# Norm writes ordered behind the next tile's residual sums, and k-interleaving kept only for the last tile of a stage head, in an eight-core encoder kernel

## The chip, the cores and the metric

The kernel runs on all 8 cores of one Trainium2 chip. Each core computes one element of the batch, and the cores exchange nothing. The metric is device time in microseconds (us) of the slowest core.

Runs come in two states. In the fast state the executions of one kernel agree within about 0.3%. In the slow state one die (four cores) or both show a lower granted TensorE clock and the time is some per cent longer; this comes and goes with any kernel. A ratio is the mean time of one kernel's fast runs over that of the other kernel's fast runs of the same rounds on the same chip, so it is not quite the ratio of the medians that are quoted. "Same" means within 2%.

Engines: PE is TensorE's matmul part, PEld its weight load, DVE is VectorE, ACT is ScalarE, POOL is GpSimd. PSUM has eight banks here, each holding one 128 x 512 fp32 block, the output of one block of matmuls.

## The reference, cut to what matters

```python
def rms_norm(x, g):
    y = x * lax.rsqrt(jnp.mean(x * x, axis=-1, keepdims=True) + EPS)
    return y * g

def sq_relu_mlp(h, w_up, w_down):               # 1024 -> 4096 -> 1024
    a = jax.nn.relu(h @ w_up)
    return (a * a) @ w_down

def short_conv_mixer(h, w_in, conv_w, w_out):   # 1024 -> 3 x 1024 -> 1024
    b, c, u = jnp.split(h @ w_in, 3, axis=-1)
    u = c * u
    # ... y = width-3 convolution of u along the sequence ...
    return (b * y) @ w_out

for i in range(2):                              # x is (8, 2048, 1024)
    h = rms_norm(x, norm_mix[i])
    x = x + (dilated_attention_mixer(h, ...) if i == 0 else short_conv_mixer(h, ...))
    x = x + sq_relu_mlp(rms_norm(x, norm_mlp[i]), *mlp_params[i])
return rms_norm(x, final_norm)
```

Every norm sits between two big matrix products: nothing of the next product can start on a token before that token's norm is done, and the norm can't start before the last residual sum of that token.

## The kernel before

Each core holds its 2048 tokens in four tiles of 512 tokens, with features on the partitions: a tile of x is eight blocks of 128 x 512 fp32 in SBUF. One output block of a 1024-wide product is eight matmuls of 128 x 512, which take about 1.73 us (8 x 216 ns) at full clock.

The kernel issues through its own list scheduler. It collects operations with their reads and writes, and places them engine by engine: of the operations that its cost model holds ready, the one with the lowest priority number, then with the lowest index. Each engine then executes in exactly that order, and waits where something isn't ready. The cost model knows durations.

```python
# in the scheduler: of the operations ready at time t on engine e
if o.ready <= t and (pick is None or (o.pri, o.idx) < (pick.pri, pick.idx)):
    pick = o
```

A norm of a tile is eight squares (on ACT, some on DVE), seven additions on GpSimd, one "ones-matmul" on PE that sums over the partitions and spreads the sum to all of them (bank 7), two activations that make the factor `rsqrt(mean + eps)`, and eight scalar_tensor_tensor instructions on DVE, `x * gain * factor`, that write the normalized tile `hT` in bf16. I call these eight "norm writes".

```python
def square_sum(gidx, src, c0, n, bank):
    for c in range(8):
        ...                                     # square of block c, on ACT or DVE
        if c:
            TT("pool", d, acc.ap[:, 0:n], o, ALU.add, ...)      # 7 adds on GpSimd, SBUF + SBUF
    MMS([(PS(bank, 0, n), onesN, h_ap(0, c0, n), True, True)], ...)   # the ones-matmul

def norm_tile(gidx, src, c0, n, bank, out_fn, pool=False, on_pe=True):
    ...
    nb_ = nrs[ni[0] % 2]
    rs = nb_.ap[:, 0:n]
    ACT(rs, PS(bank, 0, n), AF.Ln, ..., bias=eps_ap)
    ACT(rs, rs, AF.Exp, ..., scale=-0.5)        # the factor, in SBUF
    for c in range(8):
        out_fn(gidx, c, c0, n, src(c), nb_)     # norm_to_hT below, the final norm differs

def norm_to_hT(gidx, c, c0, n, src, nb_):
    STT(h_ap(c, c0, n), src[0], gain, nb_.ap[:, 0:n], ALU.mult, ALU.mult, ...)   # DVE

def add_x(tt, c, lo, n, b):                     # residual sum
    TT("dve", xa, xa, PS(b, 0, n), ALU.add, ...)    # DVE, SBUF + PSUM
```

In a stage head (the first products after a norm) each tile runs "k-interleaved": all four output blocks of the tile advance together, one 128-deep slice of `hT` after the other, so the tile can start when the first norm write is there. The price is that four of the seven banks fill at the same time and are finished at the same time.

```python
main = _Ring(range(7))                          # PSUM banks 0-6 in turn, 7 is the norm's

for tt in range(4):                             # head of the MLP
    bks = [main.next() for _ in range(4)]
    if pr == 0 and i == 0:
        for kc in range(8):
            MMS([(PS(bks[fc]), W[:, kc, ...], h_ap(kc, tt * 512, 512), kc == 0, kc == 7)
                 for fc in range(4)], ...)      # k-interleaved
    for fc in range(4):
        if pr or i:
            MMS([... for kc in range(8)], ...)  # bank by bank
        ACT(r.ap, PS(b), AF.Relu, ...)
        TT("pool", aT..., r.ap, r.ap, ALU.mult, ...)
```

Of the kernel before, what the change touches and what calls it, by code (L numbers as in the profile page):

```python
# [258 lines left out]
def build_nc():  # L259
# [22 lines left out]
    with ExitStack() as st:  # L282
# [12 lines left out]
        p = Prog()  # L295
# [26 lines left out]
        def ACT(out, in_, func, R, W, n, scale=None, bias=None, ps=True):  # L322
            kw = {}
            if scale is not None:
                kw["scale"] = scale
            if bias is not None:
                kw["bias"] = bias
            return p.op("act", lambda e: e.activation(out=out, in_=in_, func=func, **kw), R, W,  # L328
                        c_act(n, ps) + (0.09 if scale is not None and not isinstance(scale, float) else 0))
# [108 lines left out]
                    TT("pool", d, acc.ap[:, 0:n], o, ALU.add, [acc.r(0, n), r_], [dr], n)  # L438
            MMS([(PS(bank, 0, n), onesN, h_ap(0, c0, n), True, True)], [CR1, h_r(0, c0, n)], [PR(bank)])

        def norm_tile(gidx, src, c0, n, bank, out_fn, pool=False, on_pe=True):

            if not on_pe:
                square_sum(gidx, src, c0, n, bank)
            for c in range(8 if on_pe else 0):
                xa, xr = src(c)
                o, r_ = h_ap(c, c0, n), h_r(c, c0, n)
                alts = [("act", lambda e, o=o, i=xa: e.activation(out=o, in_=i, func=AF.Square), c_act(n, False)),  # L448
                        ("dve", lambda e, o=o, i=xa: e.tensor_tensor(out=o, in0=i, in1=i, op=ALU.mult),  # L449
                         c_dve(n, False))]  # L450
                if pool:
                    alts.append(("pool", alts[1][1], 0.2 + 0.0019 * n))
                p.op(alts, None, [xr], [r_], None)
                MMS([(PS(bank, 0, n), onesN, o, c == 0, c == 7)], [CR1, r_], [PR(bank)])
            nb_ = nrs[ni[0] % 2]
            ni[0] += 1
            rs = nb_.ap[:, 0:n]
            ACT(rs, PS(bank, 0, n), AF.Ln, [PR(bank), sm.r()], [nb_.r(0, n)], n, bias=eps_ap)
            ACT(rs, rs, AF.Exp, [nb_.r(0, n)], [nb_.r(0, n)], n, scale=-0.5, ps=False)
            for c in range(8):  # L460
                out_fn(gidx, c, c0, n, src(c), nb_)

        def norm_to_hT(gidx, c, c0, n, src, nb_):
            STT(h_ap(c, c0, n), src[0], sm.ap[:, S_GN + gidx * 8 + c:S_GN + gidx * 8 + c + 1],
# [416 lines left out]

        main = _Ring(range(7))

        def norm_x(gidx, tt, lo, n, fn):
            norm_tile(gidx, lambda c: xs(tt, c, lo, n), tt * 512 + lo, n, 7, fn, on_pe=n < 512)

        for tt in range(4):
            p.pri = 8000 + 10 * tt
# [22 lines left out]
        def mlp(l, base, tiles, tail):  # L911
            for pr in range(4):
                p.pri = base + 100 * pr
                fgs = (2 * pr, 2 * pr + 1)
                WU = [next_slot(wup_d[l][:, f * 512:(f + 1) * 512], 8, 512) for f in fgs]
                WD = [next_slot(wdn_d[l][f * 512:(f + 1) * 512, :], 4, 1024) for f in fgs]
                for i in range(2):
                    W, wb = WU[i]
                    for tt in range(4):
                        bks = [main.next() for _ in range(4)]  # L920
                        if pr == 0 and i == 0:
                            for kc in range(8):
                                MMS([(PS(bks[fc]), W[:, kc, fc * 128:(fc + 1) * 128], h_ap(kc, tt * 512, 512),
                                      kc == 0, kc == 7) for fc in range(4)],
                                    [wb.r(), h_r(kc, tt * 512, 512)], [PR(b) for b in bks])
                        for fc in range(4):
                            b = bks[fc]
                            if pr or i:
                                MMS([(PS(b), W[:, kc, fc * 128:(fc + 1) * 128], h_ap(kc, tt * 512, 512),
                                      kc == 0, kc == 7) for kc in range(8)],  # L930
                                    [wb.r()] + h_all(tt * 512, 512), [PR(b)])
                            r = rb_[ri[0] % 3]
                            ri[0] += 1
                            ACT(r.ap, PS(b), AF.Relu, [PR(b)], [r.r()], 512)
                            lo = fc * 2048 + tt * 512
                            TT("pool", aT[i].ap[:, lo:lo + 512], r.ap, r.ap, ALU.mult, [r.r()],
                               [aT[i].r(lo, lo + 512)], 512)
                p.pri = base + 100 * pr + 50
                for (tt, lo, n) in (tiles if pr == 3 else [(t_, 0, 512) for t_ in range(4)]):
                    c0 = tt * 512 + lo  # L940
                    for oc in range(8):
                        b = main.next()
                        MMS([(PS(b, 0, n), WD[i][0][:, fc, oc * 128:(oc + 1) * 128],
                              aT[i].ap[:, fc * 2048 + c0:fc * 2048 + c0 + n], i == 0 and fc == 0, i == 1 and fc == 3)
                             for i in range(2) for fc in range(4)],
                            [WD[0][1].r(), WD[1][1].r()] +
                            [aT[i].r(fc * 2048 + c0, fc * 2048 + c0 + n) for i in range(2) for fc in range(4)],
                            [PR(b)])
                        add_x(tt, oc, lo, n, b)
                    if pr == 3:  # L950
                        tail(tt, lo, n)

        mlp(0, 10000, [(t_, 0, 512) for t_ in range(4)], lambda tt, lo, n: norm_x(2, tt, lo, n, norm_to_hT))
# [13 lines left out]
        for i in range(8):  # L967
            p.pri = 20000 + 100 * i
            W, wb = next_slot(win_d[i], 8, 384)
            v, bs_ = vb[i % 2], bsb[i % 2]  # L970
            for tt in range(4):
                banks = [main.next() for _ in range(3)]
                parts = list(zip(banks, (128, 256, 0)))
                for ks, ps_ in ([((kc,), parts) for kc in range(8)] if i == 0 else
                                [(range(8), [q]) for q in parts]):
                    MMS([(PS(b), W[:, kc, coff:coff + 128], h_ap(kc, tt * 512, 512), kc == 0, kc == 7)
                         for (b, coff) in ps_ for kc in ks],
                        [wb.r()] + [h_r(kc, tt * 512, 512) for kc in ks], [PR(b) for (b, _) in ps_])
                cs = csb[ci % 2]
                ci += 1  # L980
                CP(cs.ap, PS(banks[0]), [PR(banks[0])], [cs.r()], 512, ("act",))
                lo = 1 + tt * 512
                TT("dve", v.ap[:, lo:lo + 512], cs.ap, PS(banks[1]), ALU.mult,
                   [cs.r(), PR(banks[1])], [v.r(lo, lo + 512)], 512)
                CP(bs_.ap[:, tt * 512:(tt + 1) * 512], PS(banks[2]), [PR(banks[2])],
                   [bs_.r(tt * 512, (tt + 1) * 512)], 512, ("act",))
            cw = [sm.ap[:, S_CW + k * 8 + i:S_CW + k * 8 + i + 1] for k in range(3)]
            for tt in range(4):
                y = yb[tt]
                o = tt * 512  # L990
                ACT(y.ap, v.ap[:, o:o + 512], AF.Copy, [v.r(o, o + 512), sm.r()], [y.r()], 512, scale=cw[0], ps=False)
                for k in (1, 2):
                    STT(y.ap, v.ap[:, o + k:o + k + 512], cw[k], y.ap, ALU.mult, ALU.add,
                        [v.r(o + k, o + k + 512), sm.r(), y.r()], [y.r()], 512)
                TT("pool", zT.ap[:, i * 2048 + o:i * 2048 + o + 512], bs_.ap[:, o:o + 512], y.ap, ALU.mult,
                   [bs_.r(o, o + 512), y.r()], [zT.r(i * 2048 + o, i * 2048 + o + 512)], 512)
        WO = [next_slot(wout_d[k * 512:(k + 1) * 512, :], 4, 1024) for k in range(2)]
        for tt in range(4):
            p.pri = 21000 + 10 * tt
            for oc in range(8):  # L1000
                b = main.next()

                def mm(kc):
                    return (PS(b), WO[kc // 4][0][:, kc % 4, oc * 128:(oc + 1) * 128],
                            zT.ap[:, kc * 2048 + tt * 512:kc * 2048 + tt * 512 + 512], kc == 0, kc == 7)

                def zr(kc):
                    return zT.r(kc * 2048 + tt * 512, kc * 2048 + tt * 512 + 512)

                MMS([mm(kc) for kc in range(7)], [WO[0][1].r(), WO[1][1].r()] + [zr(kc) for kc in range(7)], [PR(b)])  # L1010
                MMS([mm(7)], [WO[1][1].r(), zr(7)], [PR(b)])
                add_x(tt, oc, 0, 512, b)
            norm_x(3, tt, 0, 512, norm_to_hT)


# [108 lines left out]
```

## Time and profile before

| | value |
|---|---|
| time | 1524.02 us median of 3 runs (1523.65 to 1526.97) |
| span of the slowest core in the profile | 1523.8 us (core 7) |
| PE busy | 1454.9 us, 95% |
| DVE / POOL / ACT busy | 602.4 / 520.4 / 490.8 us |
| PE's share of the chain that ended last | 89% |

These are the lines of the profile's page for the kernel before: the span, the busy times, the shares of the chain that ended last, then two of the costliest groups. A group's line gives engine, operation, output<-input, shapes and count, then busy time and mean ns of one instruction, then the engine's idle time just before and its main releaser.

```profile
span 1523.8 us, 20000 instructions; the slowest of 8 cores (1516.7 to 1523.8 us)
...
PE 1454.9 (95%) x7207; PEld 674.7 (44%) x7207; DVE 602.4 (40%) x819; ACT 490.8 (32%) x778; POOL 520.4 (34%) x492
...
PE 89%; DVE 3%; DMA 3%; issue 2%; ACT 1%; POOL 1%; SPq 0%; DVEq 0%; ACTq 0%; POOLq 0%
...
L317 PE MATMUL psum<-arena 128*128 128x512 bf16 (+6 forms) x7207 | 1454.9, 366 | 61.1 <-ACT arena L448 18.3
...
L336 DVE SCALAR_TENSOR_TENSOR arena<-arena 128x512 bf16<-128x512 f32 (+2 forms) x232 | 181.6, 840 | 29.7 <-ACT arena L328 24.9
...
```

PE is the bottleneck, and it is idle for 61 us in all. L336 is 232 scalar_tensor_tensor instructions, 840 ns on average: the 136 norm writes that the change moves, 32 of the first norm and 64 of the convolution's taps. Where PE waits, once the start and the attention are over, is told by its waits between 310 and 1492 us (engine and line, what it waited for: us in total, times, longest):

```profile
...
engine line waited for: us in total, times, longest us
PE psum L317 <- ACT arena L328: 9.8, 6, 3.7
PE psum L317 <- DVE arena L333: 1.2, 1, 1.2
PE psum L317 <- POOL arena L333: 0.5, 1, 0.5
PE psum L317 <- POOL arena L965: 0.3, 1, 0.3
```

The 9.8 us behind L328 (the Relu; it frees PSUM banks) lie in the heads of the two MLPs. The timeline of the first one's head shows how they arise. A line gives start, duration, engine, line, operation and count, and in brackets the idle time before it and its releaser:

```profile
...
379.55 8.02 DVE L336 SCALAR_TENSOR_TENSOR arena<-arena 128x512 bf16<-128x512 f32 x8
...
387.49 1.27 DVE L333 TENSOR_TENSOR arena<-arena,psum 128x512 f32<-128x512 f32 x2
388.31 1.23 ACT L433 ACTIVATE arena<-arena 128x512 f32<-128x512 f32 x2 [10.09 <-DVE arena L333]
...
390.17 8.97 PE L317 MATMUL psum<-arena 128*128 128x512 bf16 x33 [2.23 <-ACT arena L328]
...
400.03 7.07 PE L317 MATMUL psum<-arena 128*128 128x512 bf16 x32 [0.90 <-ACT arena L328]
...
408.11 4.26 PE L317 MATMUL psum<-arena 128*128 128x512 bf16 x19 [1.00 <-ACT arena L328]
...
```

Read it from the top. DVE runs the eight norm writes of one tile in one block of 8.0 us (379.55). Only then come the last two residual sums of the next tile (387.49, x2). Read matmul by matmul, the products of these two sums had ended at 379.0 and 380.9 us. The squares of that tile start late accordingly (388.31, after ACT had been idle for 10.09 us). The Relus that give PE its banks back stand behind these squares in ACT's order, so PE stands for 2.23 us. The 33 matmuls after it take 8.97 us, where the 32 matmuls of the next line take 7.07: part of them ran at half clock. The waits of 0.90 and 1.00 us have another cause: the k-interleaved tile before gave back all its banks at once.

### The profile page before, as it was taken

How to read it: one execution, taken by the hardware profiler on the slowest of the kernel's cores; microseconds unless marked ns; L12 is line 12 of the kernel's file. 1: busy time of each engine (PE TensorE's matmuls, PEld its weight loads, DVE VectorE, ACT ScalarE, POOL GpSimd, SP SyncE). 2: the span in 40 equal slices, each digit the busy share in tenths (PEclk: the TensorE clock that was granted, in tenths of full speed). 3: DMA queues.
4: the chain of work that ended last, by engine and by line, in shares of the span. 5: the costliest groups of instructions: out<-in, count | busy, mean ns of one | idle time of the engine just before them, and what ended most of it. 6: DMA issues, size and time to landing. Idle time of an engine off the chain costs nothing.

```text
span 1523.8 us, 20000 instructions; the slowest of 8 cores (1516.7 to 1523.8 us)
## 1 busy us (share of the span) xinstructions
PE 1454.9 (95%) x7207; PEld 674.7 (44%) x7207; DVE 602.4 (40%) x819; ACT 490.8 (32%) x778; POOL 520.4 (34%) x492
## 2 busy tenths in 40 slices
PE   5999997699899999999999999999999999999996
PEld 2656443233344444444444444443444444444444
DVE  3646677557314013023038534457123023032057
ACT  3566686343220310310333433333310310301333
POOL 5100000135550530630665322246621621612552
PEclk8999999589999999999999999999999999999998
DMA  9944445630330420510410333311310411313014
GB/s 249 188 91 97 95 106 113 183 79 1 56 55 1 72 40 1 83 29 5 72 22 7 56 42 49 56 28 26 58 28 14 71 28 29 55 28 52 5 55 166
DMA packets 60911, 95.00 MB, mean 62 GB/s; under 512 B 3792, under 2 KB 40912, under 8 KB 58768
## 3 DMA queue, kind: packets, MB, share of 16 engines
q0 software_dynamic: 52016, 69.18, 26.6%
q1 hardware_dynamic: 8800, 24.55, 5.5%
q8 instruction: 60, 0.98, 0.3%
q14 instruction: 35, 0.29, 0.1%
HBM read 127.37 MB, written 8.52 MB: 89 GB/s over the span
## 4 chain that ended last, share of the span: by engine, by line
PE 89%; DVE 3%; DMA 3%; issue 2%; ACT 1%; POOL 1%; SPq 0%; DVEq 0%; ACTq 0%; POOLq 0%
PE psum L317 89%; DVE arena L336 3%; DMA arena<-scr 2%; DMA arena<-xT 2%; ACT arena L328 1%; DVE arena L333 1%; POOL arena L333 0%; POOL arena L349 0%; ACT arena L343 0%; ACT arena L433 0%; SPq L349 0%; DMA scr<-arena 0%; POOL arena L449 0%; DVE arena L345 0%; DVEq L216 0%
## 5 line engine op out<-in xcount | busy, mean ns | idle before, releaser
L317 PE MATMUL psum<-arena 128*128 128x512 bf16 (+6 forms) x7207 | 1454.9, 366 | 61.1 <-ACT arena L448 18.3
L317 PEld LDWEIGHTS psum<-arena 128*128 128x128 bf16 (+2 forms) x7207 | 674.7, 101 | 841.0 <-issue 155.5
L333 DVE TENSOR_TENSOR arena<-arena,psum 128x512 f32<-128x512 f32 (+1 forms) x384 | 258.2, 684 | 782.6 <-PE psum L317 776.1
L333 POOL TENSOR_TENSOR arena<-arena 128x512 bf16<-128x512 bf16 (+2 forms) x393 | 443.0, 1133 | 340.0 <-ACT arena L328 151.7
L328 ACT ACTIVATE arena<-psum 128x512 bf16<-128x512 f32 (+1 forms) x306 | 201.4, 669 | 639.0 <-PE psum L317 618.6
L336 DVE SCALAR_TENSOR_TENSOR arena<-arena 128x512 bf16<-128x512 f32 (+2 forms) x232 | 181.6, 840 | 29.7 <-ACT arena L328 24.9
L333 DVE TENSOR_TENSOR arena<-arena 128x2048 bf16<-128x2048 bf16 (+4 forms) x146 | 127.9, 921 | 35.3 <-ACT arena L328 25.7
L349 POOL DMA_DIRECT2D arena<-wdn x16 | 12.5, 784 | 318.9 <-PE psum L317 318.9
L433 ACT ACTIVATE arena<-arena 128x512 f32<-128x512 f32 x114 | 70.6, 631 | 153.4 <-DVE arena L333 136.2
L343 ACT CAST arena<-psum 128x512 bf16<-128x512 f32 (+2 forms) x149 | 87.2, 592 | 92.4 <-PE psum L317 87.7
L328 ACT ACTIVATE arena<-arena 128x512 f32<-128x512 f32 (+2 forms) x85 | 54.5, 659 | 65.3 <-DVE arena L333 51.0
L349 POOL DMA_DIRECT2D arena<-xT x18 | 13.4, 770 | 90.8 <-DVE arena L333 71.5
L349 POOL DMA_DIRECT2D arena<-wqk x8 | 7.4, 930 | 86.0 <-PE psum L317 86.0
L343 ACT COPY arena<-psum 128x512 f32<-128x512 f32 x38 | 22.9, 602 | 39.3 <-PE psum L317 39.2
L345 DVE CAST arena<-psum 128x512 bf16<-128x512 f32 (+2 forms) x27 | 18.4, 683 | 40.9 <-PE psum L317 40.7
L349 POOL DMA_DIRECT2D arena<-wup x16 | 15.0, 937 | 44.5 <-PE psum L317 39.7
L536 ACT ACTIVATE arena<-arena 128x1024 bf16<-128x1024 bf16 x23 | 24.1, 1059 | 1.9 <-DVE arena L345 0.7
L328 ACT ACTIVATE arena<-psum,arena 128x512 f32<-128x512 f32 (+1 forms) x29 | 19.5, 672 | 15.2 <-PE psum L317 14.9
L349 POOL DMA_DIRECT2D arena<-wo x8 | 4.3, 549 | 52.1 <-PE psum L317 52.1
L449 POOL TENSOR_TENSOR arena<-arena 128x512 bf16<-128x512 f32 x8 | 10.8, 1362 | 20.0 <-DMA arena<-xT 20.0
L448 ACT ACTIVATE arena<-arena 128x512 bf16<-128x512 f32 (+1 forms) x30 | 14.1, 523 | 9.2 <-DVE arena L333 7.0
L349 POOL DMA_DIRECT2D arena<-win x8 | 7.5, 932 | 14.8 <-PE psum L317 10.4
(16 smaller groups left out, 38.5 us busy)
## 6 DMA issues: line engine op xcount, KB each, us to landing
arena<-wup POOLq DMA_DIRECT2D x16, 1024.0 KB, 9.9
arena<-wdn POOLq DMA_DIRECT2D x16, 1024.0 KB, 12.8
arena<-xT POOLq DMA_DIRECT2D x14, 1024.0 KB, 9.8
arena<-arena SPq DMA_DIRECT2D x14, 512.0 KB, 4.6
arena<-scr SPq DMA_DIRECT2D x14, 512.0 KB, 6.4
arena<-win POOLq DMA_DIRECT2D x8, 768.0 KB, 7.5
outT<-arena SPq DMA_DIRECT2D x24, 256.0 KB, 2.5
arena<-wqk POOLq DMA_DIRECT2D x7, 512.0 KB, 10.0
```

What stands on the lines that cost most here:

```text
L317: i = e.matmul(o, lhsT=l, rhs=r, start=s0, stop=s1, skip_group_check=True)
L328: return p.op("act", lambda e: e.activation(out=out, in_=in_, func=func, **kw), R, W, c_act(n, ps) + (0.09 if scale is not None and not is ...
L333: return p.op(eng, lambda e: e.tensor_tensor(out=out, in0=in0, in1=in1, op=op), R, W, cost)
L336: return p.op("dve", lambda e: e.scalar_tensor_tensor(out=out, in0=in0, scalar=scalar, in1=in1, op0=op0, op1=op1), R, W, c_dve(n, False) + ...
L343: alts.append(("act", lambda e: e.copy(out=out, in_=in_), c_act(n) + more))
L345: alts.append((e_, lambda e: e.tensor_copy(out=out, in_=in_), c_dve(n, False) + more))
L349: return p.op(eng, lambda e: e.dma_start(out=out, in_=in_), R, W, 1.3 if eng == "sp" else 1.0, chan=chan, fill=fill, nbytes=nbytes)
L433: p.op([("act", lambda e, o=o, i=xa: e.activation(out=o, in_=i, func=AF.Square), c_act(n, False)), ("dve", lambda e, o=o, i=xa: e.tensor_t ...
L448: alts = [("act", lambda e, o=o, i=xa: e.activation(out=o, in_=i, func=AF.Square), c_act(n, False)), ("dve", lambda e, o=o, i=xa: e.tensor ...
L449: ("dve", lambda e, o=o, i=xa: e.tensor_tensor(out=o, in0=i, in1=i, op=ALU.mult), c_dve(n, False))]
L536: ("act", lambda e, o=sq.ap[:, sl], i_=rw.ap[:, sl]: e.activation(out=o, in_=i_, func=AF.Square), c_act(1024, False))], None, [rw.r(*rr)], ...
```

## The change

Intent: (A) the norm writes get a priority number 11 higher, so the scheduler orders them behind the next tile's residual sums; (B) only the last tile of a stage head stays k-interleaved, the other three run bank by bank, so that banks come free one at a time; (C) each tile of a down or output product gets its own priority step, which makes (A) work there too. No operation is added or removed.

```diff
-        def norm_tile(gidx, src, c0, n, bank, out_fn, pool=False, on_pe=True):
+        def norm_tile(gidx, src, c0, n, bank, out_fn, pool=False, on_pe=True, after=0):
 ...
+            p.pri += after
             for c in range(8):
                 out_fn(gidx, c, c0, n, src(c), nb_)
+            p.pri -= after
 ...
-            norm_tile(gidx, lambda c: xs(tt, c, lo, n), tt * 512 + lo, n, 7, fn, on_pe=n < 512)
+            norm_tile(gidx, lambda c: xs(tt, c, lo, n), tt * 512 + lo, n, 7, fn, on_pe=n < 512, after=11)
 ...
-                        if pr == 0 and i == 0:
+                        inter = pr == 0 and i == 0 and tt == 3
+                        if inter:
 ...
-                            if pr or i:
+                            if not inter:
 ...
-                p.pri = base + 100 * pr + 50
-                for (tt, lo, n) in (tiles if pr == 3 else [(t_, 0, 512) for t_ in range(4)]):
+                for k, (tt, lo, n) in enumerate(tiles if pr == 3 else [(t_, 0, 512) for t_ in range(4)]):
+                    p.pri = base + 100 * pr + 50 + 10 * k
 ...
                     if pr == 3:
+                        p.pri += 5
                         tail(tt, lo, n)
 ...
-                for ks, ps_ in ([((kc,), parts) for kc in range(8)] if i == 0 else
+                for ks, ps_ in ([((kc,), parts) for kc in range(8)] if i == 0 and tt == 3 else
 ...
                 add_x(tt, oc, 0, 512, b)
+            p.pri += 5
             norm_x(3, tt, 0, 512, norm_to_hT)
```

## The prediction

> **What bounds it now.** TensorE. The page shows it busy 1454.9 of 1523.8 us (95%), and 89% of the chain of waits. The change can only remove TensorE's idle time after 308 us and what follows from it. The timeline of the slowest core, read matmul by matmul, shows where that idle time is:
> - head of the first MLP (380-411 us): 2.2 + 0.9 + 1.0 = 4.1 us;
> - head of the convolution (825-842): 0.5 + 1.25 + 0.3 = 2.1 us;
> - head of the second MLP (1054-1085): 3.7 + 0.9 + 1.0 = 5.6 us;
> - the last stage: 1.1 us before the last tile's matmuls, then 14.8 us from the last down matmul (1509.1) to the end.
>
> **Why.** In each stage head VectorE runs eight scalar_tensor_tensor (0.66 us each alone, 1.7 us while a GpSimd add runs; block 379.6-387.5 us) in one block, and only then the last two residual sums of the next tile (387.5, 388.1), though their matmuls ended at 379.0 and 380.9. That tile's squares, GpSimd adds, norm and the PSUM banks wait for it. The 0.9-1.0 us gaps have another cause: a k-interleaved tile claims four of seven banks at once and finishes all four together, so the next one waits for a Relu (0.6 us). The second MLP's head also runs at half clock after its 3.7 us gap (33 matmuls take 9.8 us instead of 7.1); on five of eight cores the first MLP's does too (9.0). The Trainium skill ("TensorE: Matmul & The Clock Gate", What's actually happening) says an idle window of about 3.4 us halves the clock; this trace agrees for 3.7 us and shows it on some cores even after 2.2 us.
>
> **What the change does.** No operation is added or removed. The order of instructions shows residual sums and norm writes alternating on VectorE, the last tile's sum of squares some 6 us earlier, and tiles 0-2 of each head bank by bank. Both kinds of gap should go; the last tile still needs its norm, but 21 us of matmuls (3 x 6.9) stand before it.
>
> **Costs.** The norm writes now run among GpSimd's adds. The skill ("SBUF — State Buffer", Who interferes with whom) says a VectorE instruction with two SBUF inputs and a GpSimd one that reads SBUF exclude each other; the 0.66 against 1.7 us agrees. A pair (sum 0.6, write 0.66, wait about 0.4) comes to 1.7 us, just TensorE's 1.73 us per output block, so I expect a lag of 1-2 us, not a growing one. The small ones-matmul of the last norm is placed 5.2 us (convolution, second MLP) or 6.9 us (first MLP) into the head; my count from the trace's durations has it ready after about 4.5-5.5 us. I allow 2 us of new waits in all, at these ones-matmuls.
>
> **Sum.** Heads: 11.8 idle + about 3.5 clock. End: 1.1 (bank wait) + about 4 (the last half tile's eight sums now precede the other writes; before, VectorE reached them 4.5 us late; after, the output issues at about 0.45 us each limit). Minus 2 us. Net about 17-18 us, nearly all on the critical path, since TensorE is that path: **1506.5 us**, 8 in 10 within 1500 to 1515. Chances: faster by over 2% 0.02, within 2% 0.97, slower 0.01.
>
> **What would show it.** Right: gaps over 0.3 us at the heads nearly gone; no half clock near 390 and 1064 us; VectorE's norm writes longer on average than now (about 840 ns mean), total DVE busy up; 10-11 us from last down matmul to end; TensorE's waits on Relu (10.5 us) down to about 2.
>
> **What would make it wrong.** VectorE falling behind through the port lock: then TensorE waits at ones-matmuls, several us per head, and the gain halves. Or the end limited by output issues, giving 1 us instead of 4.

## The result, and the profile after

| | before | after |
|---|---|---|
| median of the fast runs | 1524.8 us (4 runs, 1523.65 to 1526.97) | 1522.74 us (4 runs, 1521.75 to 1523.66) |
| ratio of fast runs | | 0.9985, 95% interval 0.9967 to 1.0002 |
| spans of the eight cores in the profile | 1516.7 to 1523.8 us | 1513.7 to 1520.2 us |

The change is worth about 2 us, which the interval does not tell from nothing: same. The range of the prediction, 1500 to 1515 us, missed it. The same lines of the page, for the kernel after:

```profile
span 1520.2 us, 20021 instructions; the slowest of 8 cores (1513.7 to 1520.2 us)
...
PE 1450.2 (95%) x7207; PEld 675.1 (44%) x7207; DVE 636.2 (42%) x818; ACT 492.5 (32%) x779; POOL 526.7 (35%) x492
...
PE 88%; DVE 4%; DMA 3%; issue 2%; POOL 1%; ACT 1%; SPq 0%; POOLq 0%; DVEq 0%; ACTq 0%
...
L317 PE MATMUL psum<-arena 128*128 128x512 bf16 (+6 forms) x7207 | 1450.2, 366 | 60.4 <-DVE arena L333 15.3
...
L336 DVE SCALAR_TENSOR_TENSOR arena<-arena 128x512 bf16<-128x512 f32 (+2 forms) x232 | 221.2, 995 | 23.1 <-ACT arena L328 18.4
...
```

PE's busy time fell by 4.7 us and its idle time stayed where it was. The mean of L336 went from 840 to 995 ns, so this group keeps DVE busy 39.6 us longer with the same 232 instructions (all of DVE: 33.8 us longer). A page shows the slowest core, which is core 7 before and core 6 after, and within one execution the spans of the cores differ by over 6 us, mostly by when the first MLP begins (376.4 to 381.4 us before). So the pages are good for causes; what the change is worth is read below from one and the same core. PE's waits between 310 and 1492 us, after:

```profile
...
engine line waited for: us in total, times, longest us
PE psum L317 <- POOL arena L333: 7.4, 4, 3.0
PE psum L317 <- POOL arena L970: 3.5, 1, 3.5
```

The waits for the Relu are gone, as intended. Others of the same size have come, and all behind POOL. L333 on POOL is the last add of a tile's sum of squares; L970 is a pair of memsets that stand right behind such an add on the same engine. So PE now stands at the ones-matmuls. One place of this kind is tile 2 of the first MLP's last down pass:

```profile
...
804.12 4.36 POOL L333 TENSOR_TENSOR arena<-arena 128x512 f32<-128x512 f32 x3 [2.67 <-ACT arena L433]
...
805.70 3.33 DVE L336 SCALAR_TENSOR_TENSOR arena<-arena 128x512 bf16<-128x512 f32 x2 [1.20 <-ACT arena L328]
808.96 0.67 DVE L333 TENSOR_TENSOR arena<-arena,psum 128x512 f32<-128x512 f32 x1
809.55 0.74 DVE L336 SCALAR_TENSOR_TENSOR arena<-arena 128x512 bf16<-128x512 f32 x1
...
810.22 0.67 DVE L333 TENSOR_TENSOR arena<-arena,psum 128x512 f32<-128x512 f32 x1
810.61 2.94 POOL L333 TENSOR_TENSOR arena<-arena 128x512 f32<-128x512 f32 x2 [2.12 <-ACT arena L433]
810.81 3.29 DVE L336 SCALAR_TENSOR_TENSOR arena<-arena 128x512 bf16<-128x512 f32 x2
...
815.28 0.68 DVE L333 TENSOR_TENSOR arena<-arena,psum 128x512 f32<-128x512 f32 x1
815.68 2.94 POOL L333 TENSOR_TENSOR arena<-arena 128x512 f32<-128x512 f32 x2 [2.13 <-ACT arena L433]
...
818.76 2.10 PE L317 MATMUL psum<-arena 128*128 128x512 bf16 x9 [2.97 <-POOL arena L333]
...
```

Here DVE alternates, as the change wants: one or two norm writes of the tile before (L336), then one residual sum (L333). But look at the lengths. The single write between two sums takes 0.74 us; two writes in a row take 3.33 or 3.29 us, not 1.4. Each such pair overlaps GpSimd adds (804.12, 810.61, 815.68). The rhythm from one pair to the next is 5.07 us (the pairs start at 810.81 and, in a line left out here, at 815.88). In it DVE does two sums and three writes, and PE needs only 2 x 1.73 = 3.46 us for the two output blocks that are summed. DVE thus falls 1.6 us behind with every pair of blocks. Read instruction by instruction, the sum at 808.96 came 3.5 us after its matmuls ended and the sum at 810.22 3.1 us after; two blocks later the lags are 5.1 and 4.7 us, and 6.8 us for the first sum of the next tile. The last add of the tile ended near 818.6, and PE, which had nothing else placed before the ones-matmul, stood for 2.97 us.

It is a closed ring: a sum releases a square (0.63 us on ACT), the square releases a GpSimd add, the add holds up the norm write that runs beside it, and the write delays the next sum. That the add is what holds the write up is tested below.

Where the time went shows stage by stage. I cut each trace at the first matmul of each stage and take core 0, whose records are complete in both:

| stage (us) | before | after | difference |
|---|---|---|---|
| first MLP, up to its last down pass | 391.7 | 387.5 | -4.2 |
| its last down pass (norm of the next stage runs along) | 56.9 | 60.6 | +3.7 |
| convolution: input product and gate | 167.9 | 168.2 | +0.3 |
| convolution: output product (norm runs along) | 55.9 | 60.0 | +4.1 |
| second MLP, up to its last down pass | 394.8 | 387.5 | -7.3 |
| its last down pass (final norm runs along) | 58.6 | 64.0 | +5.4 |
| from the last down matmul to the end | 14.8 | 11.0 | -3.8 |
| sum | 1140.6 | 1138.8 | -1.8 |

The core's span fell by 1.9 us (1522.0 to 1520.1), so the table holds the whole difference. The heads and the end gave 15.3 us, and the passes in which a norm runs along took 13.5 us back. The new waits on core 0 are at six ones-matmuls: 0.39 and 0.37 us in the heads of the two MLPs, and 2.98, 2.04, 2.04 and 3.79 us, together 10.8, in the four stages that got longer. At three of these four the clock record shows half clock, for 3.4, 3.4 and 6.8 us.

The end did improve. This is PE's timeline there, before:

```profile
...
1513.93 0.27 PE L317 MATMUL psum<-arena 128*128 128x256 bf16 x1 [4.55 <-ACT arena L448]
1514.66 1.37 PE L317 MATMUL psum<-arena 128*128 128x256 bf16 x4 [0.46 <-ACT arena L448]
```

and after:

```profile
...
1496.71 13.22 PE L317 MATMUL psum<-arena 128*128 128x512 bf16 x104 [3.78 <-POOL arena L333]
1510.35 0.27 PE L317 MATMUL psum<-arena 128*128 128x256 bf16 x1 [0.42 <-ACT arena L448]
```

The gaps of 4.55 and 0.46 us in the last half tile's norm have become one of 0.42 us.

### The profile page after: what moved, and what is told of

Its sections match the earlier page's. It is cut to its first block, busy times and chain, and to the rows that moved or that the text cites. A ratio compares the mean times of both kernels' runs of the same rounds, so it can differ in the third digit from the quotient of the medians.

```text
span 1520.2 us, 20021 instructions; the slowest of 8 cores (1513.7 to 1520.2 us)
## 1 busy us (share of the span) xinstructions
PE 1450.2 (95%) x7207; PEld 675.1 (44%) x7207; DVE 636.2 (42%) x818; ACT 492.5 (32%) x779; POOL 526.7 (35%) x492
## 4 chain that ended last, share of the span: by engine, by line
PE 88%; DVE 4%; DMA 3%; issue 2%; POOL 1%; ACT 1%; SPq 0%; POOLq 0%; DVEq 0%; ACTq 0%
PE psum L317 88%; DVE arena L336 2%; DMA arena<-scr 2%; DMA arena<-xT 2%; DVE arena L333 1%; POOL arena L333 1%; ACT arena L328 1%; POOL arena L349 0%; ACT arena L343 0%; ACT arena L433 0%; SPq L349 0%; DMA outT<-arena 0%; DMA scr<-arena 0%; POOLq L282 0%; POOL arena L449 0%
## 5 line engine op out<-in xcount | busy, mean ns | idle before, releaser
L317 PE MATMUL psum<-arena 128*128 128x512 bf16 (+6 forms) x7207 | 1450.2, 366 | 60.4 <-DVE arena L333 15.3
L333 DVE TENSOR_TENSOR arena<-arena,psum 128x512 f32<-128x512 f32 (+1 forms) x384 | 259.4, 682 | 752.8 <-PE psum L317 749.0
L333 POOL TENSOR_TENSOR arena<-arena 128x512 bf16<-128x512 bf16 (+2 forms) x393 | 449.3, 1147 | 326.8 <-ACT arena L328 144.2
L336 DVE SCALAR_TENSOR_TENSOR arena<-arena 128x512 bf16<-128x512 f32 (+2 forms) x232 | 221.2, 995 | 23.1 <-ACT arena L328 18.4
L333 DVE TENSOR_TENSOR arena<-arena 128x2048 bf16<-128x2048 bf16 (+4 forms) x146 | 128.0, 921 | 35.9 <-ACT arena L328 25.1
L449 POOL TENSOR_TENSOR arena<-arena 128x512 bf16<-128x512 f32 x8 | 10.8, 1355 | 19.4 <-DMA arena<-xT 19.4
L449 DVE TENSOR_TENSOR arena<-arena 128x512 bf16<-128x512 f32 (+1 forms) x10 | 6.6, 679 | 14.9 <-DMA arena<-xT 14.7
## 6 DMA issues: line engine op xcount, KB each, us to landing
arena<-wdn POOLq DMA_DIRECT2D x16, 1024.0 KB, 11.8
```

What stands on the lines that cost most here:

```text
L317: i = e.matmul(o, lhsT=l, rhs=r, start=s0, stop=s1, skip_group_check=True)
L333: return p.op(eng, lambda e: e.tensor_tensor(out=out, in0=in0, in1=in1, op=op), R, W, cost)
L336: return p.op("dve", lambda e: e.scalar_tensor_tensor(out=out, in0=in0, scalar=scalar, in1=in1, op0=op0, op1=op1), R, W, c_dve(n, False) + ...
L449: ("dve", lambda e, o=o, i=xa: e.tensor_tensor(out=o, in0=i, in1=i, op=ALU.mult), c_dve(n, False))]
```

## The experiments

The theory after the result has two statements. First: bank by bank (B) is good and the new order (A and C) costs what it gains. Second: the order costs only because DVE and GpSimd exclude each other when both take two inputs from SBUF; without that the order would gain as well. The main rival is that something else of the order costs, such as where the ones-matmul stands in PE's queue, and that the two parts are simply worth little. Where the quoted expectations number their theories, they mean these statements in this order; "2b" is the queue place of the ones-matmul. All kernels below gave correct results. The times of before are 1525.54 us median in the first batch and 1526.18 us in the second; in each batch one run of before was slow. It is in these medians (without it they are 1525.41 and 1526.12), but left out of the ratios.

### Part B alone

```diff
# on the kernel before
-                        if pr == 0 and i == 0:
+                        inter = pr == 0 and i == 0 and tt == 3
+                        if inter:
-                            if pr or i:
+                            if not inter:
-                for ks, ps_ in ([((kc,), parts) for kc in range(8)] if i == 0 else
+                for ks, ps_ in ([((kc,), parts) for kc in range(8)] if i == 0 and tt == 3 else
```

> Only tiles 0 to 2 of each stage head run bank by bank; no priority is changed. Theory 1 (the gaps at the two MLP heads came from the four-bank claim, which asks for banks behind the late residual sums): the first MLP's stage becomes 4 to 6 us shorter, the second's 7 us, the convolution's about 1 us, no waits of over 1 us appear at the ones-matmuls of the last passes, the end stays 14.8 us after the last down matmul; about 1512 us. Rival (the head gains need the earlier residual sums of the changed kernel): only the four gaps of 0.9 to 1.0 us between interleaved tiles go, about 1520 us.

Measured: 1523.43 us (1522.8 to 1524.22), ratio 0.9987 (0.9971 to 1.0003). My first statement fails: part B alone gains nothing to speak of. PE's timeline at the first MLP's head shows what came in place of the bank waits:

```profile
...
390.84 1.89 PE L317 MATMUL psum<-arena 128*128 128x512 bf16 x8 [0.21 <-DVE arena L333]
395.64 16.64 PE L317 MATMUL psum<-arena 128*128 128x512 bf16 x68 [2.91 <-POOL arena L333]
```

The late last sums of before are still there, because the block of norm writes still precedes them, and now they are waited for at the last tile's ones-matmul (2.91 us). The second head has 2.9 us of the same, and 2.4 us at a matmul that waits for such a late sum to free its bank. Half clock of 3.4 us goes with the 2.9 us, on all eight cores at the first head and on seven at the second. The waits for the banks had hidden part of this one: taking away one of two waits in series on the same PE queue brings the other to light.

### Parts A and C alone

```diff
# on the kernel after
-                        inter = pr == 0 and i == 0 and tt == 3
+                        inter = pr == 0 and i == 0
-                for ks, ps_ in ([((kc,), parts) for kc in range(8)] if i == 0 and tt == 3 else
+                for ks, ps_ in ([((kc,), parts) for kc in range(8)] if i == 0 else
```

> Only the order behind priorities; all tiles of a head stay k-interleaved. Theory 1: it carries the cost, waits of 2 to 4 us at the ones-matmuls in the last pass of each MLP and in the convolution's output projection, and gains 4 us at the end; the 0.9 to 1.0 us gaps between interleaved tiles stay. About 1525 to 1530 us, slower than before. Rival (the two parts need each other): faster than before by 3 us or more, under 1521 us.

Measured: 1527.14 us (1526.07 to 1527.56), ratio 1.001 (0.9994 to 1.0026), and the mean of L336 is 974 ns. The waits at the ones-matmuls are those of the kernel after (3.0, 2.1 and 3.8 us among them), and the bank waits at the heads are those of before:

```profile
...
390.01 7.07 PE L317 MATMUL psum<-arena 128*128 128x512 bf16 x32 [0.84 <-ACT arena L328]
397.97 7.07 PE L317 MATMUL psum<-arena 128*128 128x512 bf16 x31 [0.89 <-ACT arena L328]
...
```

That is the cost that was expected of the order, and its gain at the end came too (11.0 us after the last down matmul). The order by itself thus gains nothing either.

### The factor of the norm left in PSUM

If exclusion is the cause, a norm write with only one input in SBUF should be free of it. The second activation writes the factor back into the norm's own bank, and the writes read it there. That occupies the bank longer, so the norm gets two banks in turn and the ring of the others shrinks to six. The order is that of the kernel after: instruction for instruction the same on DVE, ACT and POOL, and on PE too but for two groups of eight matmuls in the attention's output product, near 312 us by the scheduler's clock, that change places.

```diff
# on the kernel after
-            ACT(rs, rs, AF.Exp, [nb_.r(0, n)], [nb_.r(0, n)], n, scale=-0.5, ps=False)
+            if keep:
+                ACT(PS(bank, 0, n), rs, AF.Exp, [nb_.r(0, n)], [PR(bank)], n, scale=-0.5, ps=False)
+                nb_ = _Bank(bank)           # .ap is the PSUM bank
+            else:
+                ACT(rs, rs, AF.Exp, [nb_.r(0, n)], [nb_.r(0, n)], n, scale=-0.5, ps=False)
 ...
+            mine = set()
             for c in range(8):
+                at = len(p.ops)
                 out_fn(gidx, c, c0, n, src(c), nb_)
+                if keep:                    # eight reads of one bank by one engine need no order
+                    p.ops[at].deps -= mine
+                    mine.add(p.ops[at])
 ...
-        main = _Ring(range(7))
+        main = _Ring(range(6))
 ...
-            norm_tile(gidx, ..., n, 7, fn, on_pe=n < 512, after=11)
+            norm_tile(gidx, ..., n, 6 + nk[0] % 2, fn, on_pe=n < 512, after=11, keep=True)
+            nk[0] += 1
```

> The changed kernel, but the norm's factor stays in PSUM (two norm banks, six in the ring), so a norm write has one SBUF input and one in PSUM and should not exclude GpSimd's adds; the order on TensorE in the last passes is the same as in the changed kernel. Theory 2 (port exclusion makes VectorE late, and TensorE stands at the ones-matmuls): mean of a norm write falls from 995 to about 700 to 750 ns, the waits of 2.0 to 3.8 us at the ones-matmuls fall under 0.5 us each, half-clock stretches near 818, 1047 and 1494 us vanish; 1506 to 1510 us. Rival (the alternation of sums and writes alone makes the last sum late, lock or not): norm writes get shorter but waits of 2 us or more stay, 1519 us or more.

Measured: **1503.51 us** (1502.9 to 1505.2), ratio 0.9858 (0.9842 to 0.9873). It beats both kernels, and comes out slightly better than expected. Lines of its page:

```profile
span 1502.1 us, 20044 instructions; the slowest of 8 cores (1495.7 to 1502.1 us)
...
PE 1448.0 (96%) x7207; PEld 675.0 (45%) x7207; DVE 577.7 (38%) x818; ACT 494.7 (33%) x779; POOL 518.2 (34%) x492
...
PE 93%; DMA 3%; ACT 1%; DVE 1%; issue 1%; POOL 0%; SPq 0%; DVEq 0%; ACTq 0%; POOLq 0%
...
L336 DVE SCALAR_TENSOR_TENSOR arena<-arena,psum 128x512 bf16<-128x512 f32 (+2 forms) x136 | 90.5, 710 | 15.1 <-ACT psum L328 15.1
L336 DVE SCALAR_TENSOR_TENSOR arena<-arena 128x512 f32<-128x512 f32 (+1 forms) x96 | 70.9, 779 | 11.3 <-ACT arena L328 6.5
...
```

The 136 norm writes now read PSUM and take 710 ns (16 of them are of half length; the full ones take 742 ns, and none over 0.75); the 96 others of that line still have both inputs in SBUF and take 779 ns. If these 96 took 779 ns in the kernel after as well, its norm writes took (232 x 995 - 96 x 779) / 136 = 1147 ns there, and by the same estimate 883 ns before. (Counted one by one in the traces, on cores 3 and 7, they took 1161 to 1163 and 880 to 889 ns.) PE's share of the chain rises to 93%. PE's waits between 310 and 1492 us:

```profile
...
engine line waited for: us in total, times, longest us
PE psum L317 <- ACT arena L328: 0.4, 1, 0.4
```

One wait of 0.4 us is all that remains in 1182 us, and the clock record shows no half clock in between. DVE's timeline in the same pass as above:

```profile
...
804.75 1.40 DVE L336 SCALAR_TENSOR_TENSOR arena<-arena,psum 128x512 bf16<-128x512 f32 x2
806.07 0.68 DVE L333 TENSOR_TENSOR arena<-arena,psum 128x512 f32<-128x512 f32 x1
806.66 0.74 DVE L336 SCALAR_TENSOR_TENSOR arena<-arena,psum 128x512 bf16<-128x512 f32 x1
807.60 0.69 DVE L333 TENSOR_TENSOR arena<-arena,psum 128x512 f32<-128x512 f32 x1 [0.19 <-PE psum L317]
808.20 1.40 DVE L336 SCALAR_TENSOR_TENSOR arena<-arena,psum 128x512 bf16<-128x512 f32 x2
...
```

Two writes in a row now take 1.40 us. They overlap GpSimd adds all the same (805.76, 807.73 and 809.27, each 1.27 or 1.28 us long, are in the POOL timeline of the same stretch). DVE keeps up: some sums again wait for PE (0.19 us), as they should.

### The control: two norm banks, factor in SBUF

The experiment before changed three things: operand, ring, bank of the norm. This one changes only the last two. Its order of instructions on PE, DVE, ACT and POOL is exactly that of the kernel with the factor in PSUM.

```diff
# on the kernel after
-        main = _Ring(range(7))
+        main = _Ring(range(6))
-            norm_tile(gidx, ..., n, 7, fn, on_pe=n < 512, after=11)
+            norm_tile(gidx, ..., n, 6 + nk[0] % 2, fn, on_pe=n < 512, after=11)
+            nk[0] += 1
```

> Control: the changed kernel with six banks in the ring and two norm banks, but the factor back in SBUF. Theory 2 (the SBUF operand is what matters): as the changed kernel, 1521 to 1525 us, norm writes about 975 to 995 ns, waits of 2 to 4 us at the ones-matmuls. Rival (the second norm bank made the difference in the run with the factor in PSUM): about 1504 us.

Measured: 1523.17 us (1522.81 to 1524.62), ratio 0.9984 (0.9967 to 1.0). That is the kernel after again. Its line L336 on the page:

```profile
...
L336 DVE SCALAR_TENSOR_TENSOR arena<-arena 128x512 bf16<-128x512 f32 (+2 forms) x232 | 222.4, 1000 | 22.3 <-ACT arena L328 17.6
...
```

A mean of 1000 ns, as in the kernel after (995), so by the estimate above some 1.15 us per norm write with the factor in SBUF, against 0.71 us with it in PSUM, in the same order of instructions. So the place of one operand decides. It is not that reading PSUM is faster as such: a single full write takes 0.74 us with either operand when no GpSimd instruction runs beside it.

### Six banks alone

```diff
# on the kernel after
-        main = _Ring(range(7))
+        main = _Ring(range(6))
```

> Control for the next run: the changed kernel with six instead of seven PSUM banks in the main ring. Both theories: within 2 us of the changed kernel, 1521 to 1525 us, with the same waits at the ones-matmuls.

This one drew the slow state: 5 of 6 runs (1549.61 to 1789.06 us), the profiled one among them; the one fast run took 1522.42 us. As a time it is inconclusive. Of the four cores of the undisturbed die in the profile, three have complete matmul records; the first MLP takes 387.4 or 387.5 us there, as in the kernel after (387.5). The control above answers the question better.

### The ones-matmul placed later

The rival: only the place of the ones-matmul in PE's queue is wrong. Here the scheduler is told that it becomes ready 4.5 us later than it computes, so more matmuls of the next pass stand before it.

```diff
# on the kernel after
-            MMS([(PS(bank, 0, n), onesN, h_ap(0, c0, n), True, True)], ...)
+            MMS([(PS(bank, 0, n), onesN, h_ap(0, c0, n), True, True)], ...).late = 4.5
 ...
-                s.ready = max(s.ready, o.done + lat)
+                s.ready = max(s.ready, o.done + lat + s.late)
```

> The changed kernel with the ones-matmul of each norm placed later in TensorE's order (the scheduler believes the sum of squares to arrive 4.5 us later: two output blocks, 3.5 us, later in the last passes; a third later in the convolution's head). Nothing is taken from VectorE or GpSimd: norm writes stay near 990 ns. Theory 2b (VectorE's lateness costs only because TensorE, in order, stands at a matmul whose result nobody needs yet): the waits of 2.0 to 3.8 us fall to under 1 us, half-clock stretches there vanish, 1505 to 1511 us. Rival (VectorE is the bottleneck of the last passes; it must be waited for somewhere): the time moves to PSUM banks or the heads, 1517 us or more.

Measured: 1521.89 us (1519.63 to 1522.62), ratio 0.9971 (0.9956 to 0.9986): 0.3% better than before, within "same". The waits at the ones-matmuls are gone; the first two passes with a norm are at 55.9 us each, down from 60.6 and 60.0. But the heads of both MLPs are back at 392.2 and 393.2 us, with waits of 3.5 and 4.3 us and half clock after them. Their releaser is the norm write itself, which is L337 in this kernel, as PE's waits between 310 and 1492 us show:

```profile
...
PE psum L318 <- DVE arena L337: 8.3, 3, 4.3
...
```

DVE's timeline shows what held these writes up, at the first head:

```profile
...
388.94 11.60 DVE L337 SCALAR_TENSOR_TENSOR arena<-arena 128x512 bf16<-128x512 f32 x4
...
```

The first of these four writes takes 8.04 us alone. Seven GpSimd instructions run back to back beside it, one add and six of the MLP's squares `relu x relu`, which have their inputs in SBUF as well. At the second head one write takes 10.0 us beside nine of them (cores 1, 3 and 7), and in the kernel after, too, one write there takes 5.1 us (cores 0, 1, 3 and 7). So a write does not wait for one GpSimd instruction only: here it got its turn when GpSimd paused.

So the queue place only decides where PE meets the lag. The lag is DVE's, and it stays while the writes and GpSimd's instructions exclude each other.

### The order of before, factor in PSUM

```diff
# on the kernel before: the same edits as for the factor in PSUM above, without after=11
-            norm_tile(gidx, ..., n, 7, fn, on_pe=n < 512)
+            norm_tile(gidx, ..., n, 6 + nk[0] % 2, fn, on_pe=n < 512, keep=True)
```

> The kernel before, in its own order, with the factor in PSUM. Theory 2: the block of eight norm writes takes 5.3 instead of 7 to 8.6 us, so the first gap of each MLP head shrinks by about 1.5 us, the gaps of 0.9 to 1.0 us between interleaved tiles and the 14.8 us after the last down matmul stay about; 1517 to 1521 us. Rival (the port exclusion alone is what cost the kernel before; the order is worth nothing): 1510 us or less.

Measured: 1517.21 us (1516.71 to 1518.0), ratio 0.9943 (0.9929 to 0.9958), norm writes of 707 ns and no half clock at the heads. The scheduler's order moves in places here against before, most of all at the end (10.0 us after the last down matmul in place of 14.8, 61.0 in place of 58.6 for the pass before it), so this is not the operand alone. The operand without the change is worth about 9 us, and each MLP head keeps three bank waits of 1.33 to 1.49 us. I had expected 0.9 to 1.0; that they are longer fits the ring of six, but no run here changes the ring alone with all tiles interleaved.

### The factor in PSUM, all head tiles interleaved again

```diff
# on the kernel with the factor in PSUM
-                        inter = pr == 0 and i == 0 and tt == 3
+                        inter = pr == 0 and i == 0
-                for ks, ps_ in ([((kc,), parts) for kc in range(8)] if i == 0 and tt == 3 else
+                for ks, ps_ in ([((kc,), parts) for kc in range(8)] if i == 0 else
```

> The changed order with the factor in PSUM, but all tiles of a head k-interleaved again. Theory: the gaps of 0.84 to 1.0 us between interleaved tiles come back, three at each MLP head, 5 to 6 us in all, no other waits; 1508 to 1511 us. Rival (bank by bank is worth nothing once the sums are early): 1503 to 1505 us.

Measured: 1513.95 us (1513.66 to 1515.33), ratio 0.9923 (0.9909 to 0.9938). Bank by bank is worth about 10 us once the exclusion is gone (1513.95 against 1503.51, each with its own batch of before, whose medians differ by 0.6 us). It is more than I had expected (1508 to 1511 us for this kernel): the bank waits are 1.33, 1.38 and 1.49 us per head, against 0.84 to 1.0 us with seven banks in the ring.

### What the experiments say together

| us, median | factor in SBUF | factor in PSUM |
|---|---|---|
| order and interleaving of before | 1524.8 | 1517.21 |
| new order, interleaved as before | 1527.14 | 1513.95 |
| new order and bank by bank (the change) | 1522.74 | 1503.51 |

With the factor in SBUF, the change is worth 2 us; with the factor in PSUM, 13.7 us (1517.21 to 1503.51; these two ran in different batches, and the ratios to before of the same batch, 0.9943 and 0.9858, make it 13.0). With the factor in SBUF, neither part alone, nor both, came to more than about 2 us. The PSUM column also has six banks in the ring and two for the norm; the control shows for the last row alone that this makes no difference.

## Why the prediction was wrong

**The bottleneck and the gaps were right.** TensorE is the critical path, and the gaps that the prediction lists are those that cost. At the MLP heads after the change, gaps over 0.3 us are nearly gone: one of 0.39 and one of 0.37 us (core 0). At the convolution's head a new one of 2.04 us stands in place of the old 2.1. The half clock near 391 and 1064 us is gone on all cores but one (core 6 still has 3.4 us of it at 1063 us, behind a gap of 2.06). The waits on the Relu fell from 10.5 us to 0.8. The mean of L336 and DVE's busy time rose, as foretold (840 to 995 ns, 602.4 to 636.2 us). The end takes 11.0 us, in the foretold 10 to 11.

**The sum of the gains fits, too.** The prediction counts 11.8 + 3.5 us at the heads and 1.1 + 4 us at the end, 20.4 us in all. The kernel with the factor in PSUM, which has the same order without the exclusion, shows what the change can gain. Its stages (core 1; core 0's records are incomplete) come, in the order of the table above, to 387.0, 55.9, 166.1, 55.9, 387.0, 57.1 and 10.9 us, together 1119.9: 20.7 us under before (20.2 to 23.0 over the cores with complete records). Place by place that is 14.3 us at the heads (foretold 15.3), 2.5 in the passes with a norm (1.1) and 3.9 at the end (4). It is not shown that the order earns all of it, since the norm writes themselves are faster in this kernel.

**The step that failed is the cost:** "A pair (sum 0.6, write 0.66, wait about 0.4) comes to 1.7 us, just TensorE's 1.73 us per output block, so I expect a lag of 1-2 us, not a growing one", and from it "I allow 2 us of new waits in all". Measured, two sums and three writes take 5.07 us against PE's 3.46; the lag grows by 1.6 us with every two blocks, from 3.1 and 3.5 to 4.7 and 5.1 us and to 6.8 at the next tile. In the passes with a norm and in the convolution's head, the kernel after takes 4.7 + 2.1 + 4.1 + 6.9 = 17.8 us more than the kernel with the factor in PSUM. Of that, 10.8 us are waits at four ones-matmuls; the other 7.0 us fit the half clock that the record shows at three of them (3.4 + 3.4 + 6.8 us at half clock lose half of that, 6.8 us). So the term was 17.8 us in place of 2 (core 0; 14.7 to 17.7 on the others with complete records), and 20.4 - 17.8 = 2.6 us is near the 1.8 us that the stages of core 0 gained.

Three mistakes are in that one term. I took a wait of 0.4 us on average per write, while two of every three writes wait about 1 us (1.6 to 1.75 us in place of 0.66 to 0.74, read instruction by instruction). I treated it as independent of the rhythm, while the new order itself brings write and add together: the two sums that DVE has just finished release, over one square each, the two adds that meet the next pair of writes. And I counted no clock loss for the new waits, although I had counted it for the old ones.

**What would make it wrong** named the right mechanism ("VectorE falling behind through the port lock: then TensorE waits at ones-matmuls, several us per head, and the gain halves"). The size was off: nearly the whole gain went. Its other doubt, the output issues at the end, did not come true.

On the two places drawn from the Trainium skill: "SBUF — State Buffer", section "Who interferes with whom", says that a VectorE instruction with two SBUF inputs contends with a GpSimd instruction that reads SBUF, and that one with at most one SBUF input, outside what the page calls 2-port perf modes, does not. The runs agree on both counts: about 1.15 us (estimated above) against 0.71 us for the same norm writes in the same order. The second half of that statement was the remedy. "TensorE: Matmul & The Clock Gate", section "What's actually happening", gives an idle window of about 3.4 us for the drop to half clock. The runs agree on the length of the slow stretches (3.4 or 6.8 us), but a gap of 2.97 us was enough on seven of eight cores, and so was one of 2.04 us (near 1047 us, after).

**What stays open:** how much of the 2 us between before and after is real, since the interval of the ratio reaches 1.0002. The 17.8 us is read from one trace each of two kernels, and the split into waits and clock is a sum that fits, not an experiment of its own.

## What to carry to other kernels

When a change interleaves two engines' work more tightly, look at whether their instructions can run side by side before pricing them with durations taken alone; a lag per instruction that seems affordable grows if each delay makes the next collision, and one instruction can be held up for as long as the other engine runs without a pause (10.0 us here). Moving one operand of the VectorE instruction to PSUM, where a bank can be spared, took the collision away and turned a change worth 2 us into one worth 13. And a part of a change that shows no gain alone may still be half of a gain: waits in series on the bottleneck engine hide each other.

## What the Trainium skill lacked or had wrong

- "SBUF — State Buffer", section "Who interferes with whom", has the rule for any instruction with two SBUF inputs, but does not name scalar_tensor_tensor and gives no cost for it. Measured for 128 x 512 with two SBUF inputs: 0.74 us alone (0.66 from one to the next in a row), 1.6 to 1.75 us when it falls on a GpSimd add; 0.74 us on average with one of the two in PSUM, among the same adds. The GpSimd add is 1.27 us alone. Nor does it say who goes first when GpSimd instructions follow each other without a pause: one write stood beside nine of them for 10.0 us.
- "TensorE: Matmul & The Clock Gate", section "What's actually happening", speaks of at least one idle window of about 3.4 us. Half clock came with gaps of 2.04 us (seven of eight cores, near 1047 us, after), of 2.2 us (five of eight, first MLP's head, before) and of 2.97 us (seven of eight, after), with matmuls on both sides of the gap; another gap of 2.04 us (836.7 us, core 0, after) had none. The page doesn't say how little activity in a window counts as idle. A slow stretch of 3.4 us cost about 1.6 us (first MLP's stage before: 393.3 us on the cores with it, 391.7 on those without).
- The same page, section "Seeing it yourself", says that three or more cores of a die with dense matmuls are held at 13/16 of the clock while the load lasts. Here all eight cores run dense matmuls, and in the fast state they are granted full clock: 928 matmuls of 128 x 512 in 200 us (216 ns each) at clock 1.00 on core 0 of before from 600 to 800 us. The limit appeared only in slow executions. In the slow profile of the kernel with six banks, core 0 changes from the first to the second of these lines (stretch, us in it, busy times and counts of PE, PEld, DVE, ACT and POOL, then granted clock, DMA share and GB/s):

```profile
...
600.00:800.00 200.00, 199.05 (x910) 90.53 (x927) 44.38 (x60) 51.39 (x87) 91.35 (x86) 1.00 0.25 40
...
1000.00:1200.00 200.00, 198.67 (x748) 82.86 (x762) 73.84 (x95) 41.83 (x69) 75.88 (x67) 0.81 0.16 26
...
```

  910 matmuls recorded in 200 us at clock 1.00, then 748 at 0.81. What decides between the states, no run here shows and the page doesn't say.
